# PEER experts: the dense products over 368 tokens instead of 384, with 16 more tokens served by gathered rows

## The chip, the core and the metric

One core of a Trainium2 chip runs the whole kernel. The metric is device time in microseconds (us) of one execution, lower is better. The profile rows are from one profiled execution of the same kernel.

## What is computed

A transformer-like encoder layer over 512 tokens of width 1024. The part that matters here is its last third, the PEER expert layer. There are 128 x 128 = 16384 single-neuron experts. For each token, each of 8 heads picks 16 experts by two top-16 searches over 128 keys each:

```python
idx = jnp.take_along_axis(cand_idx, pos, axis=-1)      # 8 heads x 16 experts per token
gate = jax.nn.softmax(best, axis=-1)
...
u = w_down[ib]                                          # rows of 1024, by index
act = jax.nn.gelu(jnp.einsum('cd,chkd->chk', xb, u)) * gb
v = w_up[ib]
return jnp.einsum('chk,chkd->cd', act, v)
...
x = x + peer(rmsnorm(x, norm_ffn[l]), ...)
return rmsnorm(x, final_norm)
```

So each token needs 128 rows of `w_down` and 128 rows of `w_up`, each row 1024 float32 long.

## The kernel before

The 512 tokens are four tiles of 128. The kernel computes the experts in two ways.

**Tile 0, by rows.** `gather_init`, `fetch`, `gdown`, `gup` (L1518 to L1552). The tokens lie on the 128 partitions. For each of the 128 (head, rank) choices an indirect DMA on the POOL queue fetches 128 rows of `w_dn`, one per token (512 KB), VectorE multiplies it by the token's hidden row `h2` and sums (L1544), and later a second indirect DMA fetches 128 rows of `w_up`, which VectorE scales and adds to the sum `yg` (L1552). So there are 256 gathers of 512 KB and one VectorE instruction behind each. The rows land in four slots of the tile `area`; a new gather is issued when VectorE frees a slot.

**Tiles 1 to 3, densely, 384 tokens.** All 16384 experts are computed as 128 blocks of 128. A unit `ph1(i)` loads block i of `w_dnT` (512 KB), splits it in two float16 halves (ScalarE `whi` L453, VectorE `wlo` L456), and makes 24 matmuls with 384 moving columns into one bank (L541 to L543); ScalarE's gelu writes 128 x 384 into a slot of a ring of 35, or of the memory of `area` before the gathers need it (L1473). A unit `ph2(i)` loads block i of `w_up`, splits it in the same way, loads the gate matrix `Gb` of block i, multiplies it with the ring's slot (VectorE L1495), makes its halves `ph` (ScalarE L1496) and `pl` (VectorE L1497), and makes 18 matmuls with 512 moving columns (L1508 to L1510): three token tiles, for which `ph` and `pl` are the stationary operand, times two column halves times three. They add up in six banks `ya` over all 128 blocks.

**The gate matrices.** Between the two, `onehot` (L1408) builds for every 16 tokens the one-hot matrices `ej` and `eg` (four VectorE instructions of 128 x 2048), multiplies them on TensorE, copies the result by ScalarE into a staging tile `stg` (L1438), and writes a staging tile to HBM (`gd`) each time 64 tokens are full: six writes of 4 MB. `gload` (L1444) reads block i of it back in runs of 64 floats (256 bytes): 768 runs for each of 128 blocks.

**Order.** Three engines (TensorE, VectorE, ScalarE) run in the order in which the program emits their work; a unit's preparation (loads, halves) is emitted three units ahead of its matmuls. The stages, in us of the profiled execution: the mixers (0 to about 400); the top-16 searches of tiles 1 to 3 on VectorE beside the first `ph1` units (to about 555); the one-hot products beside about 25 further `ph1` units (to about 702); five more `ph1` units, and 14 `ph2` units alone beside the top-16 search of tile 0 (to about 784); 80 pairs of one `ph1` and one `ph2` beside the gathers (to about 1430); the last 34 `ph2` alone; the final norm.

The pace of the gathers is set by a small planner in `experts`: `tp` adds 3.95 us for each `ph1` and 3.9 for each `ph2`, `td` adds 1.14 or 2.2 for the VectorE work of the unit after next and 1.2 for each gathered row, and a gather's work is emitted while `td < tp + 1.0` and while a credit `room`, which grows by 1.65 for each unit, is at least 1. What is left is emitted at once ten units before the end:

```python
room = min(room + E.gcap, 3.0)
while td < tp + E.lead:
    ...
    elif P.yg is not None and room >= 1.0 and P.rows_left():
        P.pace(1.0)
        td += 1.2
        room -= 1.0
...
if k == len(P.units) - 10:
    P.pace(1000)
```

All loads and stores of `E.dma` are issued from one queue, SP's. Buffers: three raw tiles for `w_dnT`, two for `w_up`, three pairs of halves each, five `Gb`.

Of the kernel before, what the change touches and what calls it, by code (L numbers as in the profile page):

```python
# [46 lines left out]
def prep(x, norm_mix, w_in, q_a_norm, w_q_b, kv_a_norm, w_kv_b, w_o_attn, lam_re, lam_im, log_dt,  # L47
         b_re, b_im, c_re, c_im, d_skip, w_glu, w_o_ssm, w_out, norm_ffn, w_query, sub_keys,
         w_down, w_up, final_norm):
    c = np.ascontiguousarray  # L50
    d = {}
    x = x[0]
    d["x"] = x.reshape(4, 128, D)
    d["xT"] = c(x.T.reshape(KT, 128, T).transpose(1, 0, 2))
    col = lambda v: c(v.reshape(-1, 128).T)
    d["nmix"] = col(norm_mix[0])
    d["nq"] = col(q_a_norm[0])
    d["nkv"] = col(kv_a_norm[0])
    d["nffn_row"] = norm_ffn[0].reshape(1, D)
    d["fin_row"] = final_norm.reshape(1, D)  # L60
    w = w_in[0]
    d["w_q"] = blocks(w[:, :256], 8)
    d["w_kv"] = blocks(w[:, 256:384], 8)
    kr = w[:, 384:416]
    kr = np.concatenate([kr, kr[:, 16:], kr[:, :16]], 1)
    d["w_kr"] = c(kr.reshape(8, 128, 64).transpose(1, 0, 2))
    d["w_u"] = blocks(w[:, 416:928], 8)
    d["w_g"] = blocks(w[:, 928:], 8)
    wq = w_q_b[0].reshape(256, H, 96)
    nope = wq[:, :, :64].reshape(256, 512)  # L70
# [12 lines left out]
    d["w_up"] = w_up[0]  # L83
    d["w_dnT"] = c(w_down[0].reshape(128, 128, KT, 128).transpose(0, 3, 2, 1))
    d["lam_re"] = lanes(lam_re[0])
    d["lam_im"] = lanes(lam_im[0])
    d["logdt"] = lanes(np.broadcast_to(log_dt[0][:, :, None], (2, G, 64)))
    d["b_re"] = lanes(b_re[0])
    d["b_im"] = lanes(b_im[0])
    d["c_re"] = lanes(c_re[0].transpose(0, 1, 3, 2))  # L90
    d["c_im"] = lanes(c_im[0].transpose(0, 1, 3, 2))
    dg = np.zeros((16, G, 16), np.float32)
    dg[np.arange(16), :, np.arange(16)] = d_skip[0].reshape(G, 16).T
    dq = np.zeros((128, G // 4, 16), np.float32)
    for q in range(4):
        dq[q * 32:q * 32 + 16] = dg[:, q::4]
    d["dsk"] = dq
    d["iom"] = np.repeat(np.arange(128, dtype=np.float16), 2).reshape(1, 128, 2)
    d["io16"] = np.tile(np.repeat(np.arange(16, dtype=np.float16), 16), (128, 1)).reshape(128, 16, 16)
    pos = np.arange(T, dtype=np.float32)  # L100
    inv = (1.0 / (np.float32(10000.0) ** (np.arange(0, 32, 2, dtype=np.float32) / np.float32(32)))).astype(np.float32)
    ang = (pos[:, None] * inv[None, :]).astype(np.float32)
    cs, sn = np.cos(ang).T.astype(np.float32), np.sin(ang).T.astype(np.float32)
    d["cos"] = c(np.tile(np.concatenate([cs, cs], 0), (4, 1)) * np.float32(UNS))
    d["sin"] = c(np.tile(np.concatenate([-sn, sn], 0), (4, 1)) * np.float32(UNS))
    return {k: c(v) for k, v in d.items()}
# [951 lines left out]
def topk(E, wk, sc, ps, t):  # L1058
# [78 lines left out]
    if t == 0:  # L1137
        ix = wk.tile([128, 128], F32, name="ixf")
        V.scalar_tensor_tensor(ix, res[:, 0].rearrange("p h k -> p (h k)"), 128.0,
                               res[:, 1].rearrange("p h k -> p (h k)"), op0=OP.mult, op1=OP.add)  # L1140
        V.tensor_copy(E.gidx, ix)
        V.tensor_copy(E.ggate, res[:, 2].rearrange("p h k -> p (h k)"))
        return

    def tail():
        p = ps()
# [13 lines left out]
class Route:  # L1160
# [118 lines left out]
    def mixed_(self, t, n):  # L1279
# [74 lines left out]


class Peer:
    TD = T - 128
    NB = 128
    TS = 16
    TQ = 4  # L1360
# [37 lines left out]
        self.late = post  # L1398

    def main(self, mp, wp, gr):  # L1400
        self.wp, self.gr = wp, gr
        self.gact = mp.tile([128, 128], F32, name="gact")
        self.gco = mp.tile([128, 128], F32, name="gco")

    def sums(self, acc):
        self.ya = [[acc.tile([128, 512], F32, name=f"ya{t}{n}") for n in range(2)] for t in range(3)]
# [1 line left out]
    def onehot(self, s, op, sg):  # L1408
# [18 lines left out]

        def mm(q):
            if s * TS % TC == 0 and q == 0:
                self.stg = sg.tile([128, NB, TC], F32, name="stg", bufs=2)  # L1430
            ej, eg = tiles
            o = self.bank("")[:, :TQ * NB].rearrange("p (t i) -> p t i", i=NB)
            for t in range(TQ):
# [1 line left out]
                for i in range(2):  # L1435
                    nc.tensor.matmul(o[:, t], lhsT=ej[:, u, :, b], rhs=eg[:, i, u, :, b], start=(i == 0), stop=(i == 1))  # L1436
            t0 = (s * TS + q * TQ) % TC
            nc.scalar.copy(self.stg[:, :, t0:t0 + TQ].rearrange("p i t -> p t i"), o)  # L1438
            if t0 + TQ == TC:
                E.dma(E.gd[s * TS // TC], self.stg)  # L1440

        return prep, mm

    def gload(self, i):  # L1444
        while len(self.G) <= min(i, self.NB - 1):
            g = self.gr.tile([128, self.TD // self.TC, self.TC], F32, name="Gb", bufs=5)
            self.E.dma(g, self.E.gd.rearrange("c j i t -> j i c t")[:, len(self.G)])
            self.G.append(g.rearrange("p c t -> p (c t)"))

    def ph1(self, i, gates=None, first=None):  # L1450

# [9 lines left out]
        def mm():  # L1461
            hi, lo = w
            o = self.bank("ab"[i % 2])[:, :self.TD]
            pairs = [(hi[:, k * 128:k * 128 + 128], lo[:, k * 128:k * 128 + 128], E.hhl[:, 0, k], E.hhl[:, 1, k])
                     for k in range(KT)]
            n = len(gates or ())
            at = [1 + 5 * j // max(n - 1, 1) for j in range(n)]
            for k in range(KT):
# [11 lines left out]
    def ph2(self, i):  # L1480
# [6 lines left out]
        def prep():  # L1487
            wp = self.wp
            up, scale = E.a["w_up"][i * 128:i * 128 + 128], SP / SG
            ph = wp.tile([128, self.TD], F16, name="ph", bufs=3)  # L1490
            pl = wp.tile([128, self.TD], F16, name="pl", bufs=3)
            raw = rload(E, wp, up, D, "up")
            self.gload(i + 2)
            P = self.G[i]
            V.tensor_tensor(P, self.slot(i), P, op=OP.mult)  # L1495
            hi, lo = halves(E, wp, raw, D, "up", 3, SU, lambda: nc.scalar.activation(ph, P, AF.Copy, scale=scale))  # L1496
            V.scalar_tensor_tensor(pl, P, scale, ph, op0=OP.mult, op1=OP.subtract)  # L1497
            w.extend((hi, lo, ph, pl))

        f, l = i == 0, i == self.NB - 1  # L1500
# [17 lines left out]
    def gather_init(self):  # L1518
# [1 line left out]
        self.yg = self.area[:, 4 * D:]  # L1520
        self.nrow = 0
        E.nc.vector.memset(self.yg, 0.0)
        for g in range(9):
            for k in range(16):
                if g < 8:
                    self.gq.append((self.gdown, "w_dn", g * 16 + k))
                if g > 0:
                    self.gq.append((self.gup, "w_up", g * 16 - 16 + k))

    def fetch(self):  # L1530

        E = self.E
        while self.gq and len(self.rows) < 4:
            f, src, k = self.gq.pop(0)
            r = self.area[:, self.nrow % 4 * D:self.nrow % 4 * D + D]
            self.nrow += 1
            E.nc.gpsimd.indirect_dma_start(out=r, out_offset=None, in_=E.a[src],  # L1537
                                           in_offset=bass.IndirectOffsetOnAxis(ap=E.gidx[:, k:k + 1], axis=0))
            self.rows.append((f, k, r))

    def gdown(self, k, r):
        E = self.E
        V = E.nc.vector
        V.tensor_tensor_reduce(r, r, E.h2, op0=OP.mult, op1=OP.add, scale=1.0, scalar=0.0,  # L1544
                               accum_out=self.gact[:, k:k + 1])
        if k % 16 == 15:
            ks = slice(k - 15, k + 1)
            E.nc.scalar.activation(self.gco[:, ks], self.gact[:, ks], AF.Gelu_apprx_tanh)
            V.tensor_tensor(self.gco[:, ks], self.gco[:, ks], E.ggate[:, ks], op=OP.mult)

    def gup(self, k, r):
        self.E.nc.vector.scalar_tensor_tensor(self.yg, r, self.gco[:, k:k + 1], self.yg, op0=OP.mult, op1=OP.add)  # L1552

    def rows_left(self):
        return self.gq or self.rows
# [1 line left out]
    def pace(self, n):  # L1557
        self.owed += n
        while self.owed >= 1.0:
            self.owed -= 1.0  # L1560
            self.fetch()
            if self.rows:
                f, k, r = self.rows.pop(0)
                f(k, r)
                self.fetch()

    def final_init(self, xp):
# [63 lines left out]
def experts(E, ctx, fctx, rot, rpc):  # L1631
# [7 lines left out]
    with tc.manual_schedule(engines={eng.PE, eng.DVE, eng.Activation}):  # L1639
# [156 lines left out]
        for k in range(mid, len(P.units)):  # L1796
# [20 lines left out]
                P.final_init(cm(ctx, "fx", side="right"))  # L1817
            if k == len(P.units) - 10:
                P.pace(1000)
                for t in range(1, 4):  # L1820
                    E.dma(P.xo[t], E.x1[t])
                for n in range(2):
# [7 lines left out]
def body(tc, a, stage=None):  # L1830
# [23 lines left out]
    with ExitStack() as ctx:  # L1854
# [10 lines left out]
        E.gates = [dp.tile([8, 128, T], F32, name=f"gates{i}") for i in range(2)]  # L1865
        E.x1 = dp.tile([4, 128, D], F32, name="x1")
        E.gd = dp.tile([Peer.TD // Peer.TC, 128, Peer.NB, Peer.TC], F32, name="gd")
        E.sc0 = dp.tile([128, 2, H, 128], F32, name="sc0d")
        E.ctx = ctx
        E.R = Route(E)  # L1870
# [26 lines left out]
```

## Time and profile before

| | us |
|---|---|
| median of 3 runs | 1577.65 |
| lowest, highest | 1575.32, 1579.36 |
| the profiled execution | 1573.76 |
| its span, first to last instruction | 1571.6 |

The profiled execution is 3.9 us below the median. Busy times are of the span; matmuls are pipelined and the end of one is modelled, so successive matmuls overlap in the records and TensorE's busy share runs above its share of issued work.

### The profile page before, as it was taken

Reading aid. Unit: us, or ns where it says so; the run is one execution under the profiler, and the core shown is the slowest. Engines: PE = TensorE matmul, PEld = TensorE weight load, DVE = VectorE, ACT = ScalarE, POOL = GpSimd, SP = SyncE. Lnnn points to the kernel's source line nnn. Section 1 sums busy time; section 2 is a strip of 40 time slices with the busy share of each in tenths; the row PEclk is TensorE's granted clock in tenths of the full one; section 3 lists DMA queues with packets and bytes.
Section 4 is the critical chain, followed back from the end, with each engine's and each line's share of the span. In section 5 each row is a group of like instructions: output and inputs, shape, how many; then the busy total and the mean of one; then the engine's idle time right before and its main releaser. Section 6 shows DMA issues by size and latency. Waiting matters only on the chain. (4 is left out here: it accounts for less than half of the span.)

```text
span 1571.6 us, 26054 instructions
## 1 busy us (share of the span) xinstructions
PE 1495.3 (95%) x9865; PEld 841.2 (54%) x9865; DVE 1299.9 (83%) x2574; ACT 741.4 (47%) x1118; POOL 361.0 (23%) x300
## 2 busy tenths in 40 slices
PE   6999998789989999998999999999999999999998
PEld 3547665347676567664444555545555545544443
DVE  6888785565999999976988999898889989887556
ACT  5366766654345479873433333333333333333434
POOL 0102000000000000000025555555555555542000
PEclk9999999899999999999999999999999999999999
DMA  5532612764103347769669999999999999999763
GB/s 197 124 96 57 99 52 88 234 190 167 42 15 123 121 143 283 279 251 319 177 215 354 379 381 372 362 372 360 377 366 383 380 365 373 374 344 305 202 186 131
DMA packets 201134, 378.64 MB, mean 241 GB/s; under 512 B 112304, under 2 KB 117808, under 8 KB 199984
## 3 DMA queue, kind: packets, MB, share of 16 engines
q1 hardware_dynamic: 159904, 231.50, 44.2%
q0 software_dynamic: 39520, 142.59, 25.8%
q10 hardware_dynamic: 1584, 2.88, 0.6%
q8 instruction: 77, 1.26, 0.3%
q14 instruction: 49, 0.40, 0.1%
HBM read 340.25 MB, written 36.14 MB: 239 GB/s over the span
## 5 line engine op out<-in xcount | busy, mean ns | idle before, releaser
L456 DVE SCALAR_TENSOR_TENSOR wlo<-raw,whi 128x1024 f16<-128x1024 f32 x256 | 311.6, 1219 | 72.4 <-ACT whi L453 72.3
L453 ACT ACTIVATE whi<-raw 128x1024 f16<-128x1024 f32 x256 | 260.6, 1049 | 126.8 <-PE ya L1510 63.9
L1537 POOL DMA_INDIRECT area<-w_dn,gidx x128 | 163.5, 1278 | 672.0 <-ACT whi L453 542.8
L1508 PE MATMUL ya<-whi,ph 128*128 128x512 f16 x768 | 291.2, 379 | 3.5 <-ACT ph L1496 2.3
L1510 PE MATMUL ya<-whi,pl 128*128 128x512 f16 x768 | 291.3, 379 | 1.5
L1509 PE MATMUL ya<-wlo,ph 128*128 128x512 f16 x768 | 291.0, 379 | 1.7 <-DVE wlo L456 0.5
L1496 ACT ACTIVATE ph<-Gb 128x384 f16<-128x384 f32 x128 | 66.4, 519 | 409.4 <-DVE Gb L1495 385.9
L1537 POOL DMA_INDIRECT area<-w_up,gidx x128 | 174.5, 1363 | 152.7 <-DVE area L1552 136.4
L1552 DVE SCALAR_TENSOR_TENSOR area<-area,gco 128x1024 f32<-128x1024 f32 x128 | 164.1, 1282 | 32.2 <-DMA area<-w_up,gidx 31.7
L543 PEld LDWEIGHTS <-wlo 128*128 128x128 f16 x1272 | 124.6, 98 | 123.0 <-DVE wlo L456 21.6
L1544 DVE CUSTOM_DVE_ANT_0 area<-area,h 128x1024 f32<-128x1024 f32 x128 | 156.0, 1220 | 32.6 <-DMA area<-w_dn,gidx 32.3
L541 PEld LDWEIGHTS <-whi 128*128 128x128 f16 x1272 | 124.9, 98 | 100.9 <-ACT whi L453 5.8
L542 PEld LDWEIGHTS <-whi 128*128 128x128 f16 x1272 | 124.7, 98 | 92.2 <-issue 2.0
L1510 PEld LDWEIGHTS <-pl 128*128 128x128 f16 x768 | 75.1, 98 | 103.5 <-DVE pl L1497 15.6
L541 PE MATMUL rps<-hhl,whi 128*128 128x384 f16 x384 | 125.6, 327 | 4.0 <-ACT whi L453 4.0
L543 PE MATMUL rps<-hhl,wlo 128*128 128x384 f16 x384 | 126.0, 328 | 2.0 <-DVE wlo L456 2.0
L542 PE MATMUL rps<-hhl,whi 128*128 128x384 f16 x384 | 125.8, 328 | 0.0
L1508 PEld LDWEIGHTS <-ph 128*128 128x128 f16 x768 | 75.1, 98 | 88.7 <-ACT ph L1496 5.7
L1509 PEld LDWEIGHTS <-ph 128*128 128x128 f16 x768 | 75.1, 98 | 86.9 <-issue 1.4
L543 PE MATMUL rotb<-hhl,wlo 128*128 128x384 f16 x320 | 105.2, 329 | 4.8 <-DVE wlo L456 4.6
L543 PE MATMUL rota<-hhl,wlo 128*128 128x384 f16 x320 | 104.4, 326 | 3.9 <-DVE wlo L456 3.9
L1438 ACT COPY stg<-rps 128x512 f32<-128x512 f32 x96 | 98.2, 1075 | 16.1 <-PE rps L1436 15.2
(366 smaller groups left out, 2729.3 us busy)
## 6 DMA issues: line engine op xcount, KB each, us to landing
raw<-w_dnT SPq DMA_DIRECT2D x128, 512.0 KB
raw<-w_up SPq DMA_DIRECT2D x128, 512.0 KB
gd<-stg SPq DMA_DIRECT2D x6, 4096.0 KB
Gb<-gd SPq DMA_DIRECT2D x128, 192.0 KB
raw<-w_g SPq DMA_DIRECT2D x16, 512.0 KB
raw<-w_out SPq DMA_DIRECT2D x8, 512.0 KB
raw<-w_query SPq DMA_DIRECT2D x8, 512.0 KB
x<-x SPq DMA_DIRECT2D x8, 512.0 KB
```

The costliest lines, as they stand in the source:

```text
L453: E.nc.scalar.activation(hi, raw, AF.Copy, scale=scale)
L456: E.nc.vector.scalar_tensor_tensor(lo, raw, scale, hi, op0=OP.mult, op1=OP.subtract)
L541: E.nc.tensor.matmul(o, lhsT=lh, rhs=rh, start=start and i == 0, stop=False)
L542: E.nc.tensor.matmul(o, lhsT=lh, rhs=rl, start=False, stop=False)
L543: E.nc.tensor.matmul(o, lhsT=ll, rhs=rh, start=False, stop=stop and i == n - 1)
L1438: nc.scalar.copy(self.stg[:, :, t0:t0 + TQ].rearrange("p i t -> p t i"), o)
L1508: nc.tensor.matmul(o, lhsT=ph[:, ts], rhs=hi[:, ns], start=f, stop=False)
L1509: nc.tensor.matmul(o, lhsT=ph[:, ts], rhs=lo[:, ns], start=False, stop=False)
L1510: nc.tensor.matmul(o, lhsT=pl[:, ts], rhs=hi[:, ns], start=False, stop=l)
L1537: E.nc.gpsimd.indirect_dma_start(out=r, out_offset=None, in_=E.a[src], in_offset=bass.IndirectOffsetOnAxis(ap=E.gidx[:, k:k + 1], axis=0))
L1544: V.tensor_tensor_reduce(r, r, E.h2, op0=OP.mult, op1=OP.add, scale=1.0, scalar=0.0, accum_out=self.gact[:, k:k + 1])
L1552: self.E.nc.vector.scalar_tensor_tensor(self.yg, r, self.gco[:, k:k + 1], self.yg, op0=OP.mult, op1=OP.add)
```

## The change

The dense products cover 368 tokens. The last 16 tokens of tile 3 are served by gathered rows too, with the partitions used as 16 tokens by 8 heads: one gather fetches, for one rank k, a row for each of the 8 heads of each of the 16 tokens. So the 16 tokens take 16 gathers of `w_dn` and 16 of `w_up`.

- `ph1` multiplies 368 columns; the ring's slots, gelu, `Gb`, and the halves' work are 368 wide. `ph2` keeps 18 matmuls: `ph` and `pl` become two halves of persistent tiles `P[0..2]`, 384 wide, whose last 16 columns are set to zero once.
- The one-hot stage has 23 groups of 16 tokens instead of 24. Staging tiles hold 64 tokens five times and 48 in the last, which goes to a separate tensor `gr`; `gload` reads a block in two DMAs, 640 runs of 256 bytes and 128 of 192 bytes.
- The indices, gates and hidden rows of the 16 tokens go to HBM in the top-16 search and norm of tile 3 and come back at the end of the one-hot stage spread over 128 partitions (`xi`, `xg`, `hx`), with a selection matrix `sel`, all by the SP queue; VectorE clears `yx` and the `P` columns there.
- The new group of 16 ranks stands in the middle of the gathers' queue; there are 288 gathers. The planner's costs, its credit and its due times are the same.
- `extra()` adds the sum over heads: two float32 matmuls with 512 columns, `sel` times `yx`, into the banks of the last token tile, ten units before the end.

```diff
+TX = 16
+TD = T - 128 - TX
...
+    sel[np.arange(128), 128 - TX + np.arange(128) // 8] = SP * SU
...
+    if t == 3:
+        ix = wk.tile([128, 128], I32, name="ixi")
+        V.scalar_tensor_tensor(ix, res[:, 0].rearrange("p h k -> p (h k)"), 128.0,
+                               res[:, 1].rearrange("p h k -> p (h k)"), op0=OP.mult, op1=OP.add)
+        E.dma(E.xidx, ix[128 - TX:])
+        E.dma(E.xgate, g[128 - TX:].rearrange("p h k -> p (h k)"))
...
+        if t == 3:
+            E.dma(E.xh, h[128 - TX:])
...
 class Peer:
-    TD = T - 128
+    TD = TD
...
     def main(self, mp, wp, gr):
...
+        E.dma(self.xi, E.xidx.rearrange("a (r s) -> (a r) s", s=16))
+        E.dma(self.xg, E.xgate.rearrange("a (r s) -> (a r) s", s=16))
+        E.dma(self.hx, E.xh[:, None, :].to_broadcast([TX, 8, D]))
+        E.dma(self.sel, E.a["sel"])
+        V.memset(self.yx, 0.0)
+        self.P = [wp.tile([128, 2, 384], F16, name=f"P{i}") for i in range(3)]
+        for x in self.P:
+            V.memset(x[:, :, self.TD:], 0.0)
...
-            nc.scalar.copy(self.stg[:, :, t0:t0 + TQ].rearrange("p i t -> p t i"), o)
-            if t0 + TQ == TC:
-                E.dma(E.gd[s * TS // TC], self.stg)
+            stg = self.stg[:, :NB * self.tc].rearrange("p (i t) -> p i t", t=self.tc)
+            nc.scalar.copy(stg[:, :, t0:t0 + TQ].rearrange("p i t -> p t i"), o)
+            if t0 + TQ == self.tc:
+                E.dma(E.gd[s * TS // TC] if self.tc == TC else E.gr, stg)
...
-            self.E.dma(g, self.E.gd.rearrange("c j i t -> j i c t")[:, len(self.G)])
+            self.E.dma(g[:, :n].rearrange("p (c t) -> p c t", t=self.TC),
+                       self.E.gd.rearrange("c j i t -> j i c t")[:, len(self.G)])
+            self.E.dma(g[:, n:], self.E.gr[:, len(self.G)])
...
-            pairs = [(hi[:, k * 128:k * 128 + 128], lo[:, k * 128:k * 128 + 128], E.hhl[:, 0, k], E.hhl[:, 1, k])
-                     for k in range(KT)]
+            pairs = [(hi[:, k * 128:k * 128 + 128], lo[:, k * 128:k * 128 + 128], E.hhl[:, 0, k, :self.TD],
+                      E.hhl[:, 1, k, :self.TD]) for k in range(KT)]
...
-            ph = wp.tile([128, self.TD], F16, name="ph", bufs=3)
-            pl = wp.tile([128, self.TD], F16, name="pl", bufs=3)
+            ph, pl = (self.P[i % 3][:, x] for x in range(2))
+            phd, pld = ph[:, :self.TD], pl[:, :self.TD]
...
-        for g in range(9):
+        main = (E.h2, E.gidx, E.ggate, self.yg)
+        gs = [(main, range(g * 16, g * 16 + 16)) for g in range(8)]
+        gs.insert(4, ((self.hx, self.xi, self.xg, self.yx), range(128, 144)))
+        for a, b in zip(gs + [None], [None] + gs):
...
+    def extra(self):
+        for n in range(2):
+            ns = slice(n * 512, n * 512 + 512)
+            self.E.nc.tensor.matmul(self.ya[2][n], lhsT=self.sel, rhs=self.yx[:, ns], start=False, stop=False)
...
                 P.pace(1000)
+                P.extra()
...
+        E.gr = dp.tile([128, Peer.NB, Peer.TD % Peer.TC], F32, name="grest")
```

## Rows read from the trace of the kernel before

**Rows 1.** The page: busy time, share of the span and instructions of each engine.

```profile
PE 1495.3 (95%) x9865; PEld 841.2 (54%) x9865; DVE 1299.9 (83%) x2574; ACT 741.4 (47%) x1118; POOL 361.0 (23%) x300
```

**Rows 2.** Busy time by stage: stretch, length, engines (instructions), clock, DMA share, GB/s.

```profile
core 0: us, PE busy (x) PEld busy (x) DVE busy (x) ACT busy (x) POOL busy (x), PEclk, DMA share, GB/s
515.00:535.00 20.00, 20.00 (x123) 11.76 (x123) 20.00 (x104) 7.95 (x11) 0.00 (x0) 1.00 0.41 132
...
840.00:1424.00 584.00, 574.09 (x3054) 295.17 (x3053) 522.82 (x657) 203.98 (x298) 315.47 (x241) 1.00 1.03 370
...
1464.00:1536.00 72.00, 72.00 (x336) 32.61 (x334) 39.81 (x56) 28.95 (x41) 0.00 (x0) 1.00 0.67 190
555.00:702.00 147.00, 145.93 (x1379) 102.18 (x1377) 139.53 (x120) 126.48 (x146) 0.00 (x0) 1.00 0.61 231
702.00:730.00 28.00, 22.11 (x122) 12.13 (x123) 11.70 (x13) 11.27 (x17) 0.00 (x0) 0.94 0.99 345
```

**Rows 3.** Waits, 840 to 1424: who waited for whom, total us, times, longest.

```profile
ACT ph L1496 <- DVE Gb L1495: 349.7, 70, 8.2
...
DVE area L1552 <- DMA area<-w_up,gidx: 31.7, 34, 2.1
...
DVE area L1544 <- DMA area<-w_dn,gidx: 24.3, 28, 2.0
...
PEld L1510 <- DVE pl L1497: 12.6, 18, 0.9
```

**Rows 4.** Groups by line, 840 to 1424: the third product of `ph2`.

```profile
L1510 PE MATMUL ya<-whi,pl 128*128 128x512 f16 x438 | 166.2, 379 | 1.3
```

**Rows 5.** Timeline of TensorE: six successive `ph1` matmuls, then 25 of `ph2`.

```profile
695.07 0.33 PE L541 MATMUL rps<-hhl,whi 128*128 128x384 f16 x1
...
695.88 0.33 PE L543 MATMUL rps<-hhl,wlo 128*128 128x384 f16 x1
...
1495.63 0.38 PE L1509 MATMUL ya<-wlo,ph 128*128 128x512 f16 x1
...
1500.81 0.38 PE L1509 MATMUL ya<-wlo,ph 128*128 128x512 f16 x1
```

**Rows 6.** Timeline of VectorE: work of a gathered row, then of a `ph2` unit.

```profile
1008.26 1.28 DVE L1552 SCALAR_TENSOR_TENSOR area<-area,gco 128x1024 f32<-128x1024 f32 x1
1009.46 1.22 DVE L1544 CUSTOM_DVE_ANT_0 area<-area,h 128x1024 f32<-128x1024 f32 x1
...
1010.60 1.22 DVE L456 SCALAR_TENSOR_TENSOR wlo<-raw,whi 128x1024 f16<-128x1024 f32 x1
...
1492.22 1.23 DVE L456 SCALAR_TENSOR_TENSOR wlo<-raw,whi 128x1024 f16<-128x1024 f32 x1 [1.72 <-ACT whi L453]
1493.36 0.55 DVE L1497 SCALAR_TENSOR_TENSOR pl<-Gb,ph 128x384 f16<-128x384 f32 x1
1493.83 0.55 DVE L1495 TENSOR_TENSOR Gb<-ring,Gb 128x384 f32<-128x384 f32 x1
```

**Rows 7.** Waits in the one-hot stage, 555 to 702.

```profile
PEld L1436 <- DVE eg L1425: 6.2, 16, 0.4
...
DVE wlo L456 <- ACT whi L453: 2.3, 1, 2.3
```

**Rows 8.** Timeline after the one-hot stage: the SP queue, then TensorE.

```profile
701.75 0.33 SPq L1851 DMA_DIRECT2D gd<-stg  x1
...
715.69 1.55 SPq L1851 DMA_DIRECT2D Gb<-gd  x3
...
717.96 0.34 PE L541 MATMUL rps<-hhl,whi 128*128 128x384 f16 x1 [2.12 <-ACT whi L453]
```

**Rows 9.** DMA queue of the gathers, 840 to 1424: packets, MB, share of engines.

```profile
q0 software_dynamic: 34692, 126.32, 57.6%
```

**Rows 10.** Timeline of TensorE: float32 matmuls with 512 columns.

```profile
102.11 1.88 PE L907 MATMUL pS<-KT,QT 96*128 96x512 f32 x4
103.82 0.38 PE L927 MATMUL pT<-ident,P 128*128 128x128 f32 x2
```

More of the change, by code (lines that the diff above doesn't have):

```diff
@@ L99, in prep @@
     d["io16"] = np.tile(np.repeat(np.arange(16, dtype=np.float16), 16), (128, 1)).reshape(128, 16, 16)
+    sel = np.zeros((128, 128), np.float32)
+    sel[np.arange(128), 128 - TX + np.arange(128) // 8] = SP * SU
+    d["sel"] = sel
     pos = np.arange(T, dtype=np.float32)
@@ L1400, in main @@
     def main(self, mp, wp, gr):
+        E = self.E
+        V = E.nc.vector
         self.wp, self.gr = wp, gr
-        self.gact = mp.tile([128, 128], F32, name="gact")
-        self.gco = mp.tile([128, 128], F32, name="gco")
+        self.gact = mp.tile([128, 128 + 16], F32, name="gact")
+        self.gco = mp.tile([128, 128 + 16], F32, name="gco")
+        self.xi = mp.tile([128, 16], I32, name="xi")
+        self.xg = mp.tile([128, 16], F32, name="xg")
+        self.hx = mp.tile([128, D], F32, name="hx")
+        self.yx = mp.tile([128, D], F32, name="yx")
+        self.sel = mp.tile([128, 128], F32, name="sel")
+        E.dma(self.xi, E.xidx.rearrange("a (r s) -> (a r) s", s=16))
[6 more added lines that the diff above has]
+            V.memset(x[:, :, self.TD:], 0.0)
     def sums(self, acc):
@@ L1429, in mm @@
             if s * TS % TC == 0 and q == 0:
-                self.stg = sg.tile([128, NB, TC], F32, name="stg", bufs=2)
+                self.stg = sg.tile([128, NB * TC], F32, name="stg", bufs=2)
+                self.tc = min(TC, self.TD - s * TS)
             ej, eg = tiles
@@ L1445, in gload @@
         while len(self.G) <= min(i, self.NB - 1):
-            g = self.gr.tile([128, self.TD // self.TC, self.TC], F32, name="Gb", bufs=5)
-            self.E.dma(g, self.E.gd.rearrange("c j i t -> j i c t")[:, len(self.G)])
-            self.G.append(g.rearrange("p c t -> p (c t)"))
+            g = self.gr.tile([128, self.TD], F32, name="Gb", bufs=5)
+            n = self.TD // self.TC * self.TC
+            self.E.dma(g[:, :n].rearrange("p (c t) -> p c t", t=self.TC),
+                       self.E.gd.rearrange("c j i t -> j i c t")[:, len(self.G)])
+            self.E.dma(g[:, n:], self.E.gr[:, len(self.G)])
+            self.G.append(g)
     def ph1(self, i, gates=None, first=None):
@@ L1495, in prep @@
             V.tensor_tensor(P, self.slot(i), P, op=OP.mult)
-            hi, lo = halves(E, wp, raw, D, "up", 3, SU, lambda: nc.scalar.activation(ph, P, AF.Copy, scale=scale))
-            V.scalar_tensor_tensor(pl, P, scale, ph, op0=OP.mult, op1=OP.subtract)
+            hi, lo = halves(E, wp, raw, D, "up", 3, SU, lambda: nc.scalar.activation(phd, P, AF.Copy, scale=scale))
+            V.scalar_tensor_tensor(pld, P, scale, phd, op0=OP.mult, op1=OP.subtract)
             w.extend((hi, lo, ph, pl))
@@ L1522, in gather_init @@
         E.nc.vector.memset(self.yg, 0.0)
-        for g in range(9):
+        main = (E.h2, E.gidx, E.ggate, self.yg)
+        gs = [(main, range(g * 16, g * 16 + 16)) for g in range(8)]
+        gs.insert(4, ((self.hx, self.xi, self.xg, self.yx), range(128, 144)))
+        for a, b in zip(gs + [None], [None] + gs):
             for k in range(16):
[L1525 to L1528, printed above, removed]
+                if a:
+                    self.gq.append((self.gdown, "w_dn", a, k))
+                if b:
+                    self.gq.append((self.gup, "w_up", b, k))
     def fetch(self):
@@ L1533, in fetch @@
         while self.gq and len(self.rows) < 4:
-            f, src, k = self.gq.pop(0)
+            f, src, (s, ks), j = self.gq.pop(0)
+            k = ks[j]
             r = self.area[:, self.nrow % 4 * D:self.nrow % 4 * D + D]
@@ L1537, in fetch, with gdown @@
             E.nc.gpsimd.indirect_dma_start(out=r, out_offset=None, in_=E.a[src],
-                                           in_offset=bass.IndirectOffsetOnAxis(ap=E.gidx[:, k:k + 1], axis=0))
-            self.rows.append((f, k, r))
-    def gdown(self, k, r):
+                                           in_offset=bass.IndirectOffsetOnAxis(ap=s[1][:, k % 128:k % 128 + 1], axis=0))
+            self.rows.append((f, k, r, s))
+    def gdown(self, k, r, s):
         E = self.E
         V = E.nc.vector
-        V.tensor_tensor_reduce(r, r, E.h2, op0=OP.mult, op1=OP.add, scale=1.0, scalar=0.0,
+        V.tensor_tensor_reduce(r, r, s[0], op0=OP.mult, op1=OP.add, scale=1.0, scalar=0.0,
                                accum_out=self.gact[:, k:k + 1])
@@ L1548, in gdown, with gup @@
             E.nc.scalar.activation(self.gco[:, ks], self.gact[:, ks], AF.Gelu_apprx_tanh)
-            V.tensor_tensor(self.gco[:, ks], self.gco[:, ks], E.ggate[:, ks], op=OP.mult)
-    def gup(self, k, r):
-        self.E.nc.vector.scalar_tensor_tensor(self.yg, r, self.gco[:, k:k + 1], self.yg, op0=OP.mult, op1=OP.add)
+            V.tensor_tensor(self.gco[:, ks], self.gco[:, ks], s[2][:, k % 128 - 15:k % 128 + 1], op=OP.mult)
+    def gup(self, k, r, s):
+        self.E.nc.vector.scalar_tensor_tensor(s[3], r, self.gco[:, k:k + 1], s[3], op0=OP.mult, op1=OP.add)
+    def extra(self):
+        for n in range(2):
+            ns = slice(n * 512, n * 512 + 512)
+            self.E.nc.tensor.matmul(self.ya[2][n], lhsT=self.sel, rhs=self.yx[:, ns], start=False, stop=False)
     def rows_left(self):
@@ L1562, in pace @@
             if self.rows:
-                f, k, r = self.rows.pop(0)
-                f(k, r)
+                f, k, r, s = self.rows.pop(0)
+                f(k, r, s)
                 self.fetch()
@@ L1867, in body @@
         E.gd = dp.tile([Peer.TD // Peer.TC, 128, Peer.NB, Peer.TC], F32, name="gd")
+        E.gr = dp.tile([128, Peer.NB, Peer.TD % Peer.TC], F32, name="grest")
+        E.xidx = dp.tile([TX, 128], I32, name="xidx")
+        E.xgate = dp.tile([TX, 128], F32, name="xgate")
+        E.xh = dp.tile([TX, D], F32, name="xh")
         E.sc0 = dp.tile([128, 2, H, 128], F32, name="sc0d")
```

## Prediction, made before the changed kernel ran

> **What bounds the kernel now.** I read the page first. TensorE is busy 95% of the span [rows 1], so an edit that takes columns from it looks worth its columns. But the end of a matmul is modelled, and successive ones overlap in the records, so I counted the issued work. Six successive `ph1` matmuls are 0.162 us apart and 25 of `ph2` 0.216 us [rows 5], both 0.42 ns a column; a `ph1` of 24 takes 3.89 us and a `ph2` of 18 takes 3.885. Then I cut the span by stages, because each has its own limit [rows 2].
>
> *Top-16 searches* (the row 515 to 535): VectorE is busy 20.00 of 20 us. TensorE shows 20.00 too, but its records overlap and VectorE's hardly do, so I take VectorE as the limit here.
>
> *One-hot stage* (555 to 702): VectorE is busy 139.53 of 147 us with 120 instructions, 96 of them for the 24 groups of 16 tokens. It waits once, 2.3 us, and the weight loads of the one-hot products wait for its `eg` 16 times [rows 7]. TensorE is as full, and VectorE leads.
>
> *Pair stage* (840 to 1424): 438 of the third products are 73 `ph2` [rows 4], so 73 pairs in 584 us, 8.0 us a pair. TensorE's issued work is 73 x (3.89 + 3.885) = 568 us: 16 us are spare. VectorE is busy 522.8 us and waits 31.7 + 24.3 = 56.0 us for gathered rows [rows 2, 3]: 578.8 of 584. The list of waits tells the direction. ScalarE waits 349.7 us for VectorE's `Gb`, TensorE's weight loads wait for `pl`, and no row in this stretch names a matmul as what VectorE or ScalarE waits for. The three pairs of halves are never all full. So the stage goes at VectorE's pace, and VectorE's at that of the gathers: the DMA share is 1.03 at 370 GB/s.
>
> *Last stage*, `ph2` alone (1464 to 1536): TensorE is busy 72.00 of 72, VectorE 39.8, DMA 0.67. Only here TensorE alone sets the pace.
>
> **The change part by part.** The base is the profiled execution, 1573.76 us (its span is 1571.6), which is 3.9 below the median of 1577.65; I carry the difference over to the median.
>
> *Fewer columns in `ph1`.* 24 x 16 x 0.42 ns = 0.162 us a unit, 128 units, 20.7 us of TensorE. About 20 of the units lie beside the top-16 searches, which VectorE sets: nothing. 25 lie in the one-hot stage (below). The 80 of the pair stage are the question. If VectorE and the gathers set that stage, TensorE only waits longer. What VectorE saves there is 16 of 384 columns in `Gb` and `pl`, which hold it 0.47 us each [rows 6]: at most 0.02 us each, 0.039 a pair, 3.1 us for 80 pairs. At least nothing, if the gathers' wait takes it back. Gathers take a tenth of VectorE's time by the waits above, so I count nine tenths of it: **-2.8**. The other end, TensorE as the limit, is 80 x 0.162 = 13.0 (rival A).
>
> The reading by busy share and the reading by issued work differ here, and the Trainium skill has a rule for it ("Perfetto Trace Analysis", Identifying the Most-Contended Engine): matmul busy time is a bad measure of how close TensorE is to its limit, and the busy share of weight loads is a better one. In the pair stage matmuls show 574 of 584 us and weight loads 295 [rows 2]. Taken by the matmul share the sum would be that of rival A; by the rule it is the forecast's.
>
> *One group less in the one-hot stage.* Four VectorE instructions at 139.53/120 = 1.163 us [rows 2]: **-4.65**. TensorE drops 25 x 0.162 = 4.05 and 32 products of 128 columns (32 x 128 x 0.42 ns = 1.7), ScalarE four copies, so neither stands in the way. Should TensorE lead, it is -5.8; if the products behind the last `eg` hide some of it, -4.
>
> *After the one-hot stage.* The last staging write lasts from 701.75 to 715.69, when the first `Gb` read starts [rows 8], and a `ph1` waits 2.12 us for weights delayed by it. It shrinks by a quarter, 1.05 MB, but `hx` (0.52 MB) and `sel` (0.07) are new: 0.46 MB net at 345 GB/s [rows 2] is **-1.3**. Ends: -3.0 if the new loads go elsewhere in time, 0 if they go first. On VectorE `yx` and three strips are cleared; it is idle most of that stretch (11.7 busy of 28 [rows 2]), which hides them. If that cover fails, it is rival D.
>
> *Indices and hidden rows out.* One VectorE instruction of 128 columns in a stage that VectorE sets, under the 0.47 us of a 384-column one: **+0.2** (0 to 0.5). Three small stores join SP's queue, behind which the `w_dnT` loads wait; these are three buffers ahead, so I count nothing.
>
> *32 more gathers.* Where do they go? The credit gives 1.65 gathers a unit. By the planner's sums they begin in the 20th unit after the one-hot stage's `ph1` are done, the old 256 end two units after the last `ph1`, and the new 32 all fall into `ph2`-only units: (3.9 - 2.2)/1.2 = 1.42 a unit, so some 22 units, three units ahead of the point where all that is left would be emitted at once. The pair stage gets no gather more; the stage that TensorE sets gets them all. There VectorE needs, a unit, by the starts of successive instructions: `wlo` 1.14, `pl` 0.47, `Gb` 0.47, less 0.04: 2.04; and 32/22 = 1.45 gathered rows at (1.20 + 1.14)/2 = 1.17 [rows 6]: 1.70. Together 3.74, under 3.885. The waits decide: 56.0 us for 241 gathers (126.32 MB [rows 9] by 0.524) is 0.23 each, 0.34 a unit, 4.08 in all. The nearest row is this one, but the gate reads, slow for their bytes (share 0.67 at 190 GB/s), come twice as often as among pairs, so I raise the wait by a sixth: 4.13 us a unit, 0.245 over 3.885, x 22: **+5.4**. Bounds: nothing, if the work prepared ahead covers it (VectorE's 3.74 alone would fit). Upper, by DMA time: a unit now takes 0.67 x 16 x 3.885 = 41.6 engine-us, a gather 0.576 x 16 x 584/241 = 22.3 [rows 2, 9]; 41.6 + 1.45 x 22.3 = 74.1, over 16 engines at a share of 1.03 is 4.50 us, +13.5.
>
> *`extra()`.* Four float32 instructions with 512 columns start 0.428 us apart [rows 10], and a product shows as two of them (32 products, 64 records). Two products: **+1.7**, in the stage that TensorE sets. Its input `yx` is complete long before, since the new group stands mid-queue.
>
> *`ph` and `pl` in one tile.* If the first matmul now waits for `pl` too, it starts up to 0.47 later in units where TensorE has no lead; the third matmul waits for `pl` anyway, so nothing (at most 0.4 in 18 such waits, 7 us of TensorE's spare 16).
>
> Sum: -2.8 - 4.65 - 1.3 + 0.2 + 5.4 + 1.7 = -1.45. By the profiled execution 1572.3; by the median **1576.2 us**.
>
> **The rivals.** *A, TensorE sets the pair stage.* For it: 574 of 584 busy, and stretches like it with hardly a wait. Against it: 568 of 584 issued, and no wait on a matmul. 13.0 in place of 2.8: -11.7, **1566.0**.
>
> *B, the last gathers overload DMA.* The 22 units take 4.50 us, and the pair stage gives nothing: -4.65 - 1.3 + 0.2 + 13.5 + 1.7 = +9.4, **1587.1**. For it: DMA's share over 1 in the pair stage. Against it: by bytes a unit is 0.524 + 0.197 + 1.45 x 0.524 = 1.48 MB, at the pair stage's 370 GB/s 4.01 us. With the other terms as forecast it turns "slower" from 4.41 us a unit.
>
> *C, the reads of 192 bytes.* A gate read is 768 runs; with the weight block at no more than a gather's 22.3, it takes at least 41.6 - 22.3 = 19.3 engine-us, 25 ns a run. If a run of 192 bytes costs as much as two, 128 x 25 ns / 16 = 0.20 us a unit in the 102 units where DMA is full: +20, **1597**. The trace of before has no such run. The Trainium skill ("DMA: Bandwidth & Descriptors", How a descriptor splits into AXI transactions) says that a run which does not start on a 256-byte boundary fetches from the boundary below it; by that, part of these runs would need two transactions.
>
> *D, a stall after the one-hot stage.* The new tiles take memory that staging held. If SP's loads or VectorE's clearing wait for the last staging write, the next `ph1` starts near 712 instead of 703: +9.2 in place of -1.3, **1586.7**. Against it: they lie at the start of that memory, which is not the buffer written last.
>
> **How the numbers follow.** Chances: forecast 0.44, A 0.24, B 0.18, D 0.07, C 0.05, others 0.02. About 0.3% (4.7 us) is what a measurement can tell from no change. The forecast's own range, 1569 to 1583, gives 0.10 of its 0.44 to faster, 0.02 to slower. Of B 0.03 stays within the bound, and so do the others. Faster: 0.24 + 0.10 = 0.34; slower: 0.15 + 0.07 + 0.05 + 0.02 = 0.29; same 0.37. The range reaches from beyond A with a free last stage (1560.6) cut by a little, to just beyond B: **1562 to 1588**.
>
> **What will show it.** One-hot stage some 4.6 us shorter; the pair stage still near 8.0 us a pair, with TensorE idle more and VectorE's waits for gathers no smaller; gathers until some twelve units before the end; those units at 4.1 instead of 3.885 us with TensorE waiting for halves. Pairs at 7.85 would prove A, units at 4.4 B, gate reads with a higher DMA time C. I am wrong above all if TensorE's saving reaches the pair stage's end.

## The result, and the profile after

The changed kernel takes 1592.66 us (median of 6; before 1578.51, also of 6): the ratio of the two is 1.0099, its 95% interval 1.0077 to 1.0121. That is 14 us slower, and above the range that was given. The profiled execution took 1589.97, its span is 1588.2, 16.6 more than before.

The page's first row, beside [rows 1], shows little: TensorE 10 us less busy, VectorE 30 more, POOL 36 more.

```profile
PE 1485.0 (94%) x9837; PEld 836.1 (53%) x9837; DVE 1329.4 (84%) x2624; ACT 734.8 (46%) x1115; POOL 396.9 (25%) x332
```

The stages, as in [rows 2]: stretch, length, busy time and instructions of each engine, granted clock, DMA share, GB/s. The last row is the part of the last stage that now has gathers.

```profile
core 0: us, PE busy (x) PEld busy (x) DVE busy (x) ACT busy (x) POOL busy (x), PEclk, DMA share, GB/s
555.00:702.00 147.00, 141.81 (x1361) 101.42 (x1359) 138.87 (x122) 125.28 (x145) 0.00 (x0) 1.00 0.63 241
702.00:730.00 28.00, 24.54 (x139) 13.71 (x137) 12.77 (x33) 9.26 (x14) 0.00 (x0) 0.94 0.96 291
840.00:1424.00 584.00, 562.87 (x3044) 293.86 (x3042) 519.26 (x661) 202.63 (x299) 313.14 (x240) 1.00 1.02 367
...
1432.00:1540.00 108.00, 96.33 (x416) 38.35 (x416) 88.55 (x113) 35.89 (x50) 38.71 (x30) 1.00 0.98 315
```

In the pair stage everything is as it was but TensorE, which is busy 11 us less in the same 584 and idles that much more. In the last stage TensorE, 72.00 of 72 before, is now busy 96 of 108 us. The 416 matmuls of that stretch are 23 units, which at 3.885 us would have taken 90.

To see where the 16.6 us arose I marked the stages by their first and last instructions (the views of single tiles). "Pair stage" is from the first `ph1` matmul into the bank `rota` to the last gelu from `rotb`; "last stage" from there to the last product into `ya`.

| profiled execution of | one-hot copies | pair stage | last stage |
|---|---|---|---|
| before | 138.6 | 649.8 | 130.7 |
| changed | 134.9 | 653.1 | 148.6 |

The one-hot stage gives 3.7 us, the stretch behind it 1.7 (27.4 instead of 29.1 us from the last copy to the first `ph2` product), the pair stage nothing (it shows 3.3 more, within what single profiles differ by, see e4), and the last stage takes 17.9 more. The mark between the two stages is a gelu that starts some us behind the last matmul into `rotb`: 6.4 before, 8.4 in the changed kernel. With that matmul as the mark, the pair stages are 643.4 and 644.7 us and the last stages 137.1 and 157.0: the loss lies in the same place. Here are the last stage's two marks in the changed kernel (operation, count, durations in ns, first and last start), from the views of the tiles `rotb` and `ya`:

```profile
L1506 ACT ACTIVATE ring<-rotb x40: 456/458/460, 797.3 to 1432.5; 128x368 f32<-128x368 f32 x40
```

```profile
L1543 PE MATMUL ya<-whi,P x768: 378/379/634, 725.4 to 1581.1; 128*128 128x512 f16 x192
```

From 1432.5 to 1581.1 are the 148.6 us.

Who waits for whom in the last stage while the gathers run (1432 to 1545; total us, times, longest):

```profile
ACT whi L458 <- DMA raw<-w_up: 65.5, 24, 5.0
...
PEld L1543 <- DVE P L1530: 17.1, 17, 1.2
```

ScalarE waits for the `w_up` block in every unit, 65.5 of 113 us. Before, in the whole last stage (1424 to 1556), it waited mostly for TensorE instead:

```profile
ACT whi L453 <- PE ya L1510: 49.2, 21, 2.4
```

The chain of waits names the loop (start, length, what; 1496 to 1530):

```profile
1497.42 1.15 DVE wlo L461
1498.58 6.93 DMA raw<-w_up
...
1505.61 1.06 ACT whi L458
...
1506.70 1.24 DVE wlo L461
1507.95 6.12 DMA raw<-w_up
...
1514.18 1.07 ACT whi L458
...
1515.27 1.24 DVE wlo L461
1516.52 7.06 DMA raw<-w_up
```

`wlo` frees a raw tile, a new load into it starts at once and takes 6.93 us, ScalarE makes `whi`, VectorE `wlo`, and the tile is free again 9.37 us after (1498.58 to 1507.95). There are two such tiles for `w_up`, so a unit takes 4.68 us, whatever TensorE needs. The queue that issues the loads shows the same: from 1432 to 1540 it waits 23 times, 52.3 us in all, for a `wlo` to free a tile. The load itself is slower under the gathers (DMA issues: count, size, median us from issue to landing; first 1432 to 1540, then a stretch of `ph2` units without gathers, 720 to 780):

```profile
raw<-w_up SPq DMA_DIRECT2D x23, 512.0 KB, 6.9
```

```profile
raw<-w_up SPq DMA_DIRECT2D x13, 512.0 KB, 3.7
```

With 3.7 the loop gives about 3.1 us a unit, under 3.885; with 6.9 it sets the pace. In the pair stage a load takes 6.6 us too, but there two `w_up` tiles serve one unit in 8 us.

### The profile page after: what moved, and what is told of

It reads as the page before. It is cut to its first block, busy times and chain, and to the rows that moved or that the text cites. A ratio compares the mean times of both kernels' runs of the same rounds, so it can differ in the third digit from the quotient of the medians.

```text
span 1588.2 us, 26521 instructions
## 1 busy us (share of the span) xinstructions
PE 1485.0 (94%) x9837; PEld 836.1 (53%) x9837; DVE 1329.4 (84%) x2624; ACT 734.8 (46%) x1115; POOL 396.9 (25%) x332
## 5 line engine op out<-in xcount | busy, mean ns | idle before, releaser
L1574 POOL DMA_INDIRECT area<-w_dn,gidx x128 | 155.2, 1212 | 671.4 <-ACT whi L458 538.8
L1541 PE MATMUL ya<-whi,P 128*128 128x512 f16 x768 | 292.2, 380 | 14.6 <-ACT P L1529 14.4
L1542 PE MATMUL ya<-wlo,P 128*128 128x512 f16 x768 | 291.7, 380 | 7.6 <-DVE wlo L461 5.9
L1543 PE MATMUL ya<-whi,P 128*128 128x512 f16 x768 | 292.4, 381 | 2.7
L1529 ACT ACTIVATE P<-Gb 128x368 f16<-128x368 f32 x128 | 64.9, 507 | 423.9 <-issue 384.1
L1543 PEld LDWEIGHTS <-P 128*128 128x128 f16 x768 | 75.1, 98 | 120.8 <-DVE P L1530 34.4
L1541 PEld LDWEIGHTS <-P 128*128 128x128 f16 x768 | 75.1, 98 | 105.3 <-ACT P L1529 26.3
L546 PE MATMUL rps<-hhl,whi 128*128 128x368 f16 x384 | 123.8, 322 | 4.6 <-ACT whi L458 4.6
L548 PE MATMUL rps<-hhl,wlo 128*128 128x368 f16 x384 | 124.1, 323 | 3.6 <-DVE wlo L461 3.1
L547 PE MATMUL rps<-hhl,whi 128*128 128x368 f16 x384 | 123.8, 322 | 0.0
L1542 PEld LDWEIGHTS <-P 128*128 128x128 f16 x768 | 75.2, 98 | 84.0 <-issue 1.2
L548 PE MATMUL rotb<-hhl,wlo 128*128 128x368 f16 x320 | 102.3, 320 | 7.4 <-DVE wlo L461 7.3
L548 PE MATMUL rota<-hhl,wlo 128*128 128x368 f16 x320 | 102.2, 319 | 5.1 <-DVE wlo L461 5.1
L546 PE MATMUL rotb<-hhl,whi 128*128 128x368 f16 x320 | 102.2, 319 | 0.6 <-ACT whi L458 0.6
```

Source lines behind the costliest of these rows:

```text
L546: E.nc.tensor.matmul(o, lhsT=lh, rhs=rh, start=start and i == 0, stop=False)
L547: E.nc.tensor.matmul(o, lhsT=lh, rhs=rl, start=False, stop=False)
L548: E.nc.tensor.matmul(o, lhsT=ll, rhs=rh, start=False, stop=stop and i == n - 1)
L1541: nc.tensor.matmul(o, lhsT=ph[:, ts], rhs=hi[:, ns], start=f, stop=False)
L1542: nc.tensor.matmul(o, lhsT=ph[:, ts], rhs=lo[:, ns], start=False, stop=False)
L1543: nc.tensor.matmul(o, lhsT=pl[:, ts], rhs=hi[:, ns], start=False, stop=l)
```

## The experiments

T1 is the theory just read from the chain: the loop of load and halves through two tiles. Rivals: T2, the DMA engines are simply full (share 0.98); T3, the gate reads in two DMAs with runs of 192 bytes. For the pair stage, theory P says that VectorE and the gathers set it, rival A that TensorE does.

**e1: five raw tiles in the last stage.** In `ph2`:

```diff
-            raw = rload(E, wp, up, D, "up")
+            raw = rload(E, self.dp, up, D, "dn") if i > 93 and i % 2 else rload(E, wp, up, D, "up")
```

> The changed kernel, but once the last ph1 is done every second w_up block is loaded into the three raw tiles that w_dnT no longer needs: five raw tiles instead of two; nothing else differs. Theory T1 (in the last stage each load of a w_up block takes 5.6 to 7.3 us under the gathers, and with two raw tiles a unit cannot be shorter than half of load plus halves, (6.9 + 1.06 + 1.24 + some waiting)/2 = 4.7 us): with five tiles the units fall to about 4.1 us, the time to 1592.7 - 23 x 0.6 = about 1579. Theory T2 (the DMA engines are full there, share 0.98, and more tiles only queue more): no change, 1589 to 1594. Theory T3 (the gate reads in two DMAs with 192-byte runs cost the time): no change either.

Measured: 1576.21 us (before on the same chip 1579.72), ratio 0.9984, interval 0.9958 to 1.001. The loss is gone. The last stage takes 131.4 us, with all 32 gathers and the two float32 products in it. The stretch with gathers, by engines:

```profile
1432.00:1520.00 88.00, 87.93 (x408) 39.47 (x407) 84.53 (x111) 33.49 (x47) 40.44 (x31) 1.00 1.07 365
```

TensorE is full again (87.93 of 88), VectorE nearly. The same DMA engines that moved 315 GB/s at a share of 0.98 now move 365. ScalarE's `whi`, which waited for a load in every unit, waits for none from 1432 to 1520. T1 holds, T2 falls.

**e2: the cut without its gathers.** In `gather_init`:

```diff
-        gs.insert(4, ((self.hx, self.xi, self.xg, self.yx), range(128, 144)))
```

> The changed kernel without the new group of gathers (the last 16 tokens get no expert output; their two float32 products add zeros). All that the dense cut saves, and none of the 32 gathers. If the loss lies in the gathers of the last stage (T1 and T2), that stage goes back to 3.885 us a unit and the time is 1592.7 - 18 = about 1574.5, 4 below the kernel before, the pair stage still at 8.1 us a pair. If the gate reads cost it (T3), the last stage stays above 4.1 us a unit and the time above 1585. If TensorE's shorter ph1 were worth its 13 us in the pair stage, it would be 1564.

Measured: 1577.79 (before 1579.72), ratio 0.9989, 0.9963 to 1.0014; last stage 132.7, pair stage 654.5. The gathers of the last stage carry the loss. The cut alone, with 20.7 us of `ph1` columns removed and no gather to pay, saves 2 us in the medians where I expected 4; the interval holds both, and not the 13 of rival A.

**e3: the gates read as before.** Six chunks of 64, written and read as in the kernel before, and one DMA. The part that reads:

```diff
...
-            n = self.TD // self.TC * self.TC
-            self.E.dma(g[:, :n].rearrange("p (c t) -> p c t", t=self.TC),
-                       self.E.gd.rearrange("c j i t -> j i c t")[:, len(self.G)])
-            self.E.dma(g[:, n:], self.E.gr[:, len(self.G)])
...
+            self.E.dma(g, self.E.gd.rearrange("c j i t -> j i c t")[:, len(self.G)])
...
```

> The changed kernel with the gate matrices staged, written and read as before: six chunks of 64 tokens (the last 16 columns zero), one read of 768 runs of 256 bytes for each block. The last staging write is 4.2 MB again, which may cost up to 3 us after the one-hot stage. T3 (two DMAs and 192-byte runs): the last stage and the pair stage get faster, 1585 or less. T1 and T2: 1592 to 1596.

Measured: 1597.5 (before 1579.72), ratio 1.0111, 1.0064 to 1.0157; last stage 149.5. No faster: T3 falls.

**e4: the kernel before with five raw tiles.** The edit of e1.

> The kernel before with the five raw tiles of e1 in its last stage. Control: that stage has no gathers and TensorE sets it at 3.885 us a unit, so T1 expects no change, 1577 to 1580. If more raw tiles help by themselves (a smoother entry into the last stage), it would be up to 2 us less.

Measured: 1582.09 (before 1579.72), ratio 1.0018, 0.9994 to 1.0041. That is 2 us above the range expected, but the interval includes no change. Tiles alone bring nothing. Its pair stage, whose code is that of before, shows 658.3 us where the profiled execution of before shows 649.8: single profiles of this stage differ by some 8 us.

**e5: the kernel before, five raw tiles, fewer gathers among the pairs.** The edit of e1, and the credit:

```diff
-    E.lead, E.gcap = 1.0, 1.65
+    E.lead, E.gcap = 1.0, 1.45
```

> The kernel before (384 dense tokens, 256 gathers) with five raw tiles in the last stage and a credit of 1.45 gathers a unit instead of 1.65: 224 of the 256 gathers in the pair stage instead of 254, the other 32 in the last stage. Theory P (VectorE and the gathers set the pair stage, 1.17 us of work and 0.23 of waiting for each gather, until TensorE's 7.78 us a pair is reached): the pair stage loses the 20 to 28 us that it stands above TensorE's time, the last stage keeps 3.9 us a unit as in e1, the time is 1555 to 1562. Rival A (TensorE sets the pair stage): no change, 1578 to 1582.

Measured: 1553.16 (before 1580.82), ratio 0.9829, 0.9805 to 0.9853. The pair stage takes 624.0 us, 26 less with the same matmuls. Some 6 of these are the mark: the last gelu now starts 0.3 us behind the last matmul into `rotb` and not 6.4. By that matmul it is 623.7 for 643.4, 20 less. The waits in it (840 to 1400) turn round:

```profile
ACT ring L1473 <- PE rotb L543: 71.0, 32, 2.9
ACT ring L1473 <- PE rota L543: 68.5, 31, 2.9
...
DVE area L1544 <- DMA area<-w_dn,gidx: 5.3, 11, 0.8
DVE area L1552 <- DMA area<-w_up,gidx: 3.9, 5, 1.5
```

Now ScalarE's gelu waits for TensorE 63 times, which it never did from 840 to 1424 in the kernel before, and VectorE's waits for gathers fall from 53.5 us in this stretch to 9.2. Theory P holds, rival A falls. P names VectorE and the gathers together, and no run here separates them: each gather that moves takes its VectorE work and its transfer along.

e5 also bears on T1. Where gathers run in its last stage (1410 to 1510) a `w_up` load takes 8.7 us (median of 25), longer than the 6.9 of the changed kernel, and TensorE is still full: with five tiles the latency no longer counts.

**e6: the same credit, two raw tiles.**

> As e5, but with the two raw tiles of the kernel before. Theory P and T1 together: the pair stage gains 20 to 28 us and the last stage gives back 18 by its load loop, as in the changed kernel: 1570 to 1580, with units of 4.6 to 4.7 us while gathers run. If the loop were not the cause, it would equal e5.

Measured: 1560.42 (before 1580.82), ratio 0.9875, 0.9851 to 0.9899. Better than expected. The pair stage gains as in e5 (626.5). The last stage shows 145.2 us, 14.5 more than before, but 6 of these are the mark again: by the last matmul into `rotb` it is 145.6, for 137.1 before and 136.0 in e5. So the loop costs some 9 us here, not 18, and by the medians e6 is 7.3 above e5 (the profiled execution is the slowest of five, 1568.1). Loads land in 5.6 us there (median, 1432 to 1530), and the loop is shorter for it.

**e7: the change with five tiles and a credit of 1.6.**

> The changed kernel with five raw tiles in the last stage (e1) and a credit of 1.6: 247 gathers in the pair stage instead of 254, 38 in the last stage, 3 emitted at once ten units before the end. Theory P: 7 x 1.4 = 10 us less than e1, 1564 to 1570. Rival A: as e1, 1575 to 1578.

Measured: 1576.12 (before 1580.82), ratio 0.9972, 0.9949 to 0.9994: no better than e1, so the sum was wrong. The pair stage does lose 13 us against e1 (640.2 for 653.4), and the last stage takes as much more (144.1 for 131.4). It does not lose them unit by unit: from 1425 to 1525 TensorE is busy 99.56 of 100 us beside a VectorE busy 94.13. Then it stops once, for 9.13 us (1528.5 to 1537.6). The last rows, emitted at once, and the first tile's final norm hold VectorE from 1522.4 to 1536.5, and the next unit's work stands behind them.

**e8: the cut where TensorE sets the pairs.** e5's edits on the changed kernel, with e2's.

> The changed kernel with five raw tiles in the last stage, without the new group of gathers (the last 16 tokens get no expert output) and with a credit of 1.45: e5 with the dense cut on top. It prices the cut where VectorE no longer sets the pairs. Theory P: TensorE now sets them, so the 0.162 us of each of 80 ph1 arrive, 13 us, and 4.7 of the one-hot stage, less 1.7 for the two float32 products: 1540 to 1546, some 16 below e5. If TensorE's columns are worth nothing there either (DMA sets the pairs), it is 3 to 4 below e5.

Measured: 1539.03 (before 1580.82), ratio 0.9745, 0.9718 to 0.9772, 14.1 below e5 and just under the range expected. TensorE is full in both, first e5, then e8:

```profile
840.00:1420.00 580.00, 580.00 (x3122) 305.33 (x3121) 505.75 (x642) 217.00 (x307) 301.51 (x217) 1.00 1.02 359
```

```profile
840.00:1420.00 580.00, 580.00 (x3174) 310.36 (x3173) 516.28 (x658) 220.87 (x315) 300.78 (x223) 1.00 1.03 366
```

Since matmul records overlap, the full share alone would not prove it. The pace does: 624.0 us are 7.80 a pair, for 7.775 of issued work. And here the columns arrive: 610.9 us of pair stage instead of 624.0, the 13 us that 80 x 0.162 promises.

**e9 and e10: the whole change, five tiles, credits of 1.45 and 1.5.**

> The whole change (368 dense tokens, 288 gathers) with five raw tiles in the last stage and a credit of 1.45: 224 gathers in the pair stage, 38 in the last stage, 26 emitted at once ten units before the end. It puts the cut beside e5 with its gathers paid. Theory P (a gather costs VectorE 1.17 us wherever it is put; VectorE has no 37 us to spare): the pair stage runs at TensorE's time as in e8, the 26 rows take VectorE 31 us at a point where ten units can hide 18 of them, so 1539 + 5 + 13 = 1550 to 1560, no better than e5 (1553). Rival (the gathers are free once the load loop is open): 1541 to 1545.

> As e9 with a credit of 1.5: 232 gathers in the pair stage, 18 emitted at once. Theory P: the pair stage close to TensorE's time with some waits of it on VectorE, 1550 to 1560 again, since what leaves one stage arrives in another. Rival: 1541 to 1545.

Measured: 1590.26 (before 1578.68; ratio 1.0082, 1.005 to 1.0113) and 1578.83 (1.0001, 0.9984 to 1.0018). Both miss. The pair stages are fine (613.2 and 613.8, TensorE full), the last stages are not (189.9 and 174.3). I had counted the rows emitted at once as work that ten units hide. TensorE's timeline of e9 shows why they don't:

```profile
1553.54 0.61 PE L1541 MATMUL ya<-whi,P 128*128 128x512 f16 x1 [49.31 <-ACT P L1529]
...
1554.98 0.63 PE L1541 MATMUL ya<-whi,P 128*128 128x512 f16 x1
1555.41 0.63 PE L1542 MATMUL ya<-wlo,P 128*128 128x512 f16 x1
```

VectorE runs in the order of emission. 26 rows in a block, and the first tile's final norm, stand ahead of every later unit's `Gb` and halves, VectorE waits 17.2 us for rows in between, and TensorE runs dry for 49 us. That costs a little more than the stop itself: the granted clock falls to 0.50 (1.2 instead of 2.4 GHz) while TensorE idles, and the matmuls behind the stop start 0.43 us apart instead of 0.216 until about 1559.5, some 3 us.

**e11: e5 with a credit of 1.5.**

> e5 (384 dense tokens, 256 gathers, five raw tiles) with a credit of 1.5: 232 gathers in the pair stage, 24 in the last. Theory P: the pair stage still at TensorE's time, the last stage up to 3 us shorter than in e5: 1549 to 1555. If the pairs of e5 stood just at VectorE's limit, 8 more gathers cost 8 x 1.4 = 11 us: 1564.

Measured: 1553.74 (before 1578.68), ratio 0.9845, 0.9823 to 0.9867; pair stage 624.8, last stage 135.6. As e5: 232 gathers still fit beside the pairs.

**e12: the whole change, spread best.** Five tiles, a credit of 1.55, and:

```diff
-            if k == len(P.units) - 10:
+            if k == len(P.units) - 6:
```

> The whole change with five raw tiles, a credit of 1.55, and the point where what is left of the gathers is emitted at once (with the first tile's final norm) moved from ten to six units before the end: 239 gathers in the pair stage, 45 in the last, 4 at once. The best spread that the planner gives the 288 gathers. If the cut only needed room for its gathers, it reaches 1540 to 1550, below e5 (1553). If a gathered row costs VectorE its 1.17 us plus waiting wherever it stands (theory P), it stays above e5: 1555 to 1568.

Measured: 1568.7 (before 1579.91), ratio 0.9928, 0.9902 to 0.9955; pair stage 627.9, last stage 149.5. The best that I found with the cut is 15 us above e5 without it, and just above the range of theory P. But the last stage does not show a price that each row pays. First a part before the rows emitted at once, then the part with them:

```profile
1410.00:1480.00 70.00, 69.92 (x325) 31.47 (x323) 67.36 (x94) 26.13 (x37) 32.08 (x26) 1.00 1.06 361
1490.00:1550.00 60.00, 44.64 (x191) 19.00 (x190) 50.20 (x63) 19.41 (x30) 24.08 (x16) 0.86 0.86 292
```

TensorE is full until the block of the last rows and the final norm, and there it stops once, for 15.26 us, as in e7 and e9; the clock falls to 0.50 again, which costs some 2 us more. Without the stop e12 would stand at about 1551 (an estimate: 1568.7 - 15.3 - 2.2), beside e5's 1553. No run spreads those rows over the last units.

## Why the prediction was wrong

**32 more gathers, +5.4: the step that failed.** They fell where it said, into the `ph2`-only units, 34 rows in some 23 units. The price was mis-sized, and so was its upper bound: a unit took 4.68 us where 4.13 was forecast, and the last stage took 17.9 us more, of which `extra()` is 1.7, so 16.2 where 5.4 was taken and 13.5 allowed. I asked what VectorE and what the DMA engines can carry in a unit. The limit was a latency: a load that lands after 6.9 us instead of 3.7, in a loop through two tiles. The bound by DMA share, 4.50 us a unit, came near the size by luck and had the wrong cause, as e1 shows: with five tiles the same traffic fits at 3.885 us a unit. The prediction had no term for the loop at all, though the number of raw tiles was in the code.

**Pair stage, -2.8.** It gave nothing that can be seen, within the 8 us by which single profiles differ. The direction was right: VectorE and gathers set it, and 13 us of TensorE vanished there. e5 shows it from one side (30 gathers fewer, 20 to 26 us shorter by the two marks), e8 from the other (the 13 us arrive once TensorE is the limit). VectorE's waits for gathers stayed, 56.6 us in 840 to 1400 (the four rows below) for 53.5 before:

```profile
DVE area L1589 <- DMA area<-w_up,gidx: 27.9, 27, 3.8
DVE area L1581 <- DMA area<-w_dn,gidx: 18.7, 26, 2.1
DVE area L1581 <- DMA area<-w_dn,xi: 5.5, 5, 2.0
DVE yx L1589 <- DMA area<-w_up,xi: 4.5, 4, 1.7
```

The rule of the Trainium skill ("Perfetto Trace Analysis", Identifying the Most-Contended Engine) to judge TensorE by the busy share of weight loads and not of matmuls pointed the right way here. But its number hardly tells the cases apart: weight loads are 295 of 584 us where TensorE was not the limit [rows 2] and 305 of 580 in e5, where it is. What told them apart was who waits for whom.

**One-hot stage, -4.65.** 3.7 by the first and last copy, 138.6 to 134.9 (135.0 in e1, 134.9 in e2, 138.5 in e4). That is less than four instructions at 1.163 us, and less than the near end that I gave (4); where the missing us stays was not tried.

**Indices and hidden rows out, +0.2:** too small to see. The first one-hot copy starts at 562.1 us before and at 562.7 after, at 560.7 in e1 and 563.6 in e2.

**After the one-hot stage, -1.3:** 1.7. VectorE's clearing of `yx` did wait 5.0 us for a staging write, as rival D feared, but in time in which it would have been idle.

**`extra()`, +1.7:** right. The four instructions start at 1548.41 and the next product at 1550.12, 1.71 us later. The gathers are done by then and TensorE is full again, so these us count.

**Rivals.** A is refuted by e2 and e5. B had the place, not the mechanism. C: the Trainium skill ("DMA: Bandwidth & Descriptors", How a descriptor splits into AXI transactions) says that a run which does not start on a 256-byte boundary also fetches the bytes below its start; e3, with runs of 256 bytes alone, is no faster. D cost nothing. That the first product waits for both halves in one tile was not tried by itself.

**What the cut is worth.** 16 tokens take 13 us of columns and 3.7 of one-hot work out, where TensorE is the limit. They put in 32 rows of 1.17 us on VectorE, 37 us, in stages where VectorE is busy 87% (e5's pairs) to 96% (e1's last stage). The changed kernel is slower for the load loop, which e1 shows. That it is no faster with the loop open has two parts. In e1 the pairs still go at the pace of VectorE and the gathers (653.4 us), so the columns do not arrive; e2, e5 and e8 show that. With fewer gathers among the pairs (e7, e9, e10, e12) the time goes into one stop of TensorE, 9 to 49 us, where the last rows are emitted in a block. Whether the cut with its gathers could pass e5 if that block were spread stays open; by the estimate at e12 there is little to win.

## What to carry to other kernels

Before adding a stream to a stage, draw the buffer loops of the loads that are there: tiles x unit time must exceed the load's latency under the new traffic plus the work that frees the tile; a loop with spare time at 3.7 us of latency was the limit at 6.9. A busy share near 1 does not say by itself who sets a stage: look for which engine's work the others wait for, and move work out of that stage. Do not emit a block of work on an engine that has no lead there: it stopped TensorE for 9 to 49 us in four of these runs. Here 30 gathers moved to the last stage, with raw tiles that lay idle there, gave 1.7% where removing 20 us of matmul columns gave nothing.

## What the hardware showed unexpectedly

The DMA share is no measure of room here: 0.98 at 315 GB/s in the changed kernel's last stage, 1.07 at 365 GB/s in e1 with about the same bytes a unit (1.47 and 1.42 MB). A 512 KB load takes 3.7 us beside gate reads alone and 6.9 beside gathers, although the engines then move 315 GB/s and could move 365. With more tiles it takes longer still, 8.7 us in e5, and nothing waits for it.
